# An encoder block on one core: value products of 256 columns in the attention, a smaller tile ring, the gated unit by token halves, and gate stores on another queue

## The chip, the cores and the metric

One core of a Trainium2 chip runs the whole program once. The metric is the device time of that execution in microseconds (us); lower is better. PE is the matrix engine, ACT the scalar engine, DVE the vector engine, POOL the GpSimd engine, SP the engine that here only issues DMAs. ACT and POOL issue DMAs too, each from its own instruction stream.

## The reference

```python
h = h + 0.5 * swiglu(rms_norm(h, g1), wg1, wu1, wd1)              # 1024 tokens x 1024
z = rms_norm(h, gm) @ w_in
q, k, v, s_in, gates = split(z)                                  # 512 each, gates 2 x 1024
y_attn = neighbourhood_attention(q, k, v, rpb) @ w_attn_out      # 8 heads, 16 x 64 grid, window 8 x 16
y = s5_scan(s_in, forward) + s5_scan(s_in, backward) + D * s_in  # diagonal state space
y = gelu(y); y_ssm = (y * sigmoid(y @ glu_w + glu_b)) @ w_ssm_out
h = h + (sigmoid(gates[0]) * y_attn + sigmoid(gates[1]) * y_ssm) @ w_out
h = h + 0.5 * swiglu(rms_norm(h, g2), wg2, wu2, wd2)
h = h + (p @ w_proj) * sigmoid(rms_norm(h, g3) @ w_gate)
return rms_norm(h, gf)
```

## The kernel before, in words

All products of weights are made from operands split into a high and a low part: `split` copies the value rounded (ACT, L159) and subtracts it (DVE, L160), and `mm3` issues three products of 512 columns (L190, L191, L192). A weight tile so split is called wh and wl.

The program is written as one main stream of such products and one side generator. After each `mm3` the main stream calls `tick()`; when the number that the generator last yielded has run down, the generator writes its next piece into the program. So `yield 3` means that three `mm3` of the main stream stand between two pieces. PE executes in the order written. The orders of ACT, DVE, POOL and SP are set by the scheduler of the compiling layer, which sorts by a simulated timeline; the build fixes them, and each engine then works through its list.

The first feed-forward layer ends near 685 us and the second one begins near 1327 us. Between them lies the mixer. Its main stream is the projection of q, k and the gates, 84 steps `s_run` of 12 products each (banks px, py, pz), in twelve groups of seven. A step needs a weight tile blk (loaded by a DMA on ACT's queue) as wh and wl. Results leave by `s_evac` into tiles z, and `s_out` stores the gates from z to g_d: four stores for each group of gates, on ACT's queue.

The generator `mixer_side` writes, in this order: the injection of the state-space input; the scan; the attention; the products that turn states into outputs (yo); the gated unit (glu).

The scan is 128 steps of three POOL instructions each (L1154, L1155, L1156), which depend on each other and on nothing else after the injection. `scan_steps` only writes them down; `scan["c"]` counts the steps that are written, not those that POOL has done.

The attention is 64 units, numbered 0 to 63 here, (head, row block, column block), in a loop over j. Iteration j writes the scores of unit j (bank s, tile sm), the three transpositions of unit j - 2 (`attn_turn`, bank pt), the value products of unit j - 4 (`attn_values`, bank O), then `yield 3`. The transposed weights are kept as a high part ph and a low part pl, two tiles of 384 columns. For each of three row groups, two value products of 128 columns are issued: v (high and low side by side, 128 columns of weights) times ph, and v's high part (64 columns) times pl. Four units share a bank O. When the fourth is in, ACT copies its lower half to ol (L1261), DVE adds (L1262) and the sum ot goes to o_d.

Tiles come from rings. Ring m has 24 buffers of 128 x 512 and holds blk, wh, wl, z, queries, values, ot, ol, y and more. Ring a has 12 buffers of 128 x 384 and holds sm, ph, pl, the bias tables tb, and before and after the attention the loads of the state-space products (ut, fmi, emi). A tile that takes a buffer waits until the last user of the buffer is done; if that was a store, until the store has landed.

After the attention, for each of 16 pairs, `ssm_load` brings emi (two DMAs) and ut; `ssm_out` copies states to xs, issues the yo products (L1180, L1182), copies them to ys (ACT, L1184) and stores them to y_d by two DMAs of POOL's queue (L1187). The gated unit works in two halves of the positions s: `glu_load` brings four tiles yt, each with half the positions of one channel quarter m, `glu_act` applies gelu in place on ACT, `glu_half` splits weight and yt to wgl, yh and yl and issues 12 products per quarter, then sigmoid and product give sg, stored to y2_d (named y_d in the rows). Every half needs all quarters, so the first half waits for the last pair of the state-space part.

At the end of the mixer `load_br` brings o_d and y2_d back by token halves t for the products br. The y2_d loads pick 64 of 128 chunks: runs of 256 bytes.

Of the kernel before, what the change touches and what calls it, by code (L numbers as in the profile page):

```python
# [16 lines left out]
P = 128  # L17
SEQ = 1024
# [23 lines left out]
def encoder_block(ctx, tc, I, out):  # L42
# [79 lines left out]
    o_d = dtile("o_d", [512, SEQ])  # L122
    g_d = dtile("g_d", [16, P, SEQ])
    y_d = dtile("y_d", [4, P, L, NCH])
    y2_d = dtile("y2_d", [512, SEQ])
    f_d = dtile("f_d", [NPAIR, P, 512])
    e_d = dtile("e_d", [NPD, P, 384])

# [937 lines left out]
    cur.update(st=(ap_, "k4", 2), w=(ap_, "m", NM), tmp=(ap_, "m", NM))  # L1066

    def ta(name, shape=(P, 384), dt=F32):
        return ap_.tile(list(shape), dt, tag="a", bufs=12, name=name)

    def proj(w, t, name):
        o = bank(name)
# [130 lines left out]
    def load_q(hd, rb):  # L1203
        hp, i = hd // 2, hd % 2
        qs[hd, rb] = [tmp("q" + n, dt=F32R) for n in "hl"]
        for a in range(2):
            for s_ in halves2:
                nc.sync.dma_start(qs[hd, rb][a][s_].bitcast(F32), q_d[hp, a, halves2[i], hsl(rb)])

    def load_v(hd, cb):  # L1210
        n = 4 * KNC[cb]
# [28 lines left out]
    def attn_turn(cb, sm):  # L1240
        kp = 4 * KNC[cb]
        tp = bank("pt")
        for g in range(3):
            T.transpose(tp[0:kp, ksl(g)], sm[:, g * kp:(g + 1) * kp], ident)
        ph, pl = ta("pth", dt=F32R), ta("ptl", dt=F32R)
        A.copy(ph[0:kp], tp[0:kp, 0:384])
        V.tensor_tensor(pl[0:kp], tp[0:kp, 0:384], ph[0:kp].bitcast(F32), ALU.subtract)
        return ph, pl

    def attn_values(hd, rb, cb, O, ph, pl):  # L1250
        kp = 4 * KNC[cb]
        hl = vld[hd, cb]
        for g in range(3):

            T.matmul(O[:, ksl(cb)], lhsT=hl[0:kp, rb + g], rhs=ph[0:kp, ksl(g)], start=(g == 0), stop=False,
                     skip_group_check=True)
            T.matmul(O[0:64, ksl(cb)], lhsT=hl[0:kp, rb + g, 0:64], rhs=pl[0:kp, ksl(g)], start=False, stop=(g == 2),
                     skip_group_check=True)
        if cb == 3:
            ot, ol = tmp("ot"), tmp("ol")  # L1260
            A.copy(ol[0:64], O[64:128])  # L1261
            V.tensor_tensor(ot[0:64].rearrange("p (r b c) -> p b r c", r=8, b=4),  # L1262
                            O[0:64].rearrange("p (b r c) -> p b r c", b=4, r=8),
                            ol[0:64].rearrange("p (b r c) -> p b r c", b=4, r=8), ALU.add)
            late.append((o_d[hd * 64:(hd + 1) * 64, hsl(rb)], ot[0:64]))


    ygs = {}

    def glu_load(t):  # L1270
        for m in range(4):
            yt = ygs[t, m] = tmp("yt")
            nc.sync.dma_start(yt, y_d[m, :, 4 * t:4 * t + 4].rearrange("p t c -> p (t c)"))

    def glu_act(t):
        for m in range(4):
            A.activation(ygs[t, m], ygs[t, m], AF.Gelu_apprx_tanh)
# [6 lines left out]
    def glu_w(raw):  # L1284
        w = ap_.tile([P, 2, HT], F32R, tag="k4", bufs=2, name="wgl")
        split(w[:, 0], w[:, 1], raw)
        return w

    def glu_half(t, raws):
        os_ = [bank("glu") for _ in range(4)]  # L1290
        for k in range(4):
            w = glu_w(raws.pop(0))
            y = tmp("yh", dt=F32R), tmp("yl", dt=F32R)
            split(*y, ygs[t, k])
            if 4 * t + k < 6:
                raws.append(glu_raw((k + 2) % 4))
            yield 2
            for m in range(4):
                mm3(os_[m], (w[:, 0, ksl(m)], w[:, 1, ksl(m)]), y, k == 0, k == 3)
        for m in range(4):  # L1300
            sg = tmp("sg")
            A.activation(sg, os_[m], AF.Sigmoid, bias=glub[:, m:m + 1])
            V.tensor_tensor(sg, sg, ygs.pop((t, m)), ALU.mult)
            nc.scalar.dma_start(y2_d[ksl(m), hsl(t)], sg)
        yield 2

    stored, ready = set(), set()
    SO = 56
# [1 line left out]
    def mixer_side():  # L1310
        yield from u_second()
        while 3 not in stored:
            yield 1
        yield 7
        new_x()
        ld = {}
        for pr in range(3):
            ld[pr] = inject_load(pr)
        yield 10
        for pr in range(NPAIR):  # L1320
            if pr + 3 < NPAIR:
# [17 lines left out]
        load_q(0, 0)  # L1339
        for _ in range(6):  # L1340
            scan_steps(1)
            yield 2
        sms, pts, O = {}, {}, {}
        late.clear()
        lo, so = {}, {}
        for j in range(n + 5):
            if j < n:
                hd, rb, cb = units[j]
                b = 2 * hd + rb
                load_tab(b + cb // 2, (1, 2, 0, 0)[cb]) if cb < 3 else None  # L1350
                if cb == 1 and rb == 0:
                    load_q(hd, 1)
                if cb == 1 and rb == 1 and hd + 1 < NH:
                    while hd + 1 not in ready:
                        yield 1
                    load_q(hd + 1, 0)
                if rb == 0 and cb == 2 and hd + 1 in ready:
                    load_k(hd + 1)
                if rb == 1 and cb == 2 and hd + 1 < NH and hd + 1 not in khl:
                    load_k(hd + 1)  # L1360
                sms[j] = attn_scores(hd, rb, cb)
            if 0 <= j - 2 < n:
                pts[j - 2] = attn_turn(units[j - 2][2], sms.pop(j - 2))
            while late:
                nc.scalar.dma_start(*late.pop())
            if 0 <= j - 4 < n:
                hd, rb, cb = units[j - 4]
                if cb == 0:
                    O[hd, rb] = bank("O")
                attn_values(hd, rb, cb, O[hd, rb], *pts.pop(j - 4))  # L1370
# [7 lines left out]
        scan_steps(NCH)  # L1378
        for p in range(NPAIR + 1):
            if 3 <= p + 3 < NPAIR:  # L1380
                lo[p + 3] = ssm_load(p + 3)
            if p < NPAIR:
                so[p] = ssm_out(p, *lo.pop(p))
            if p > 0:
                so.pop(p - 1)()
            yield 1 + p % 2
        yield 3
        glu_load(0)
        raws = [glu_raw(0), glu_raw(1)]
        yield 11  # L1390
        glu_act(0)
        glu_load(1)
        yield 2
        glu_act(1)
        for t in range(2):
            yield from glu_half(t, raws)

    start(mixer_side())

# [58 lines left out]
    def load_br(t, b):  # L1458

        res = []  # L1460
        if b == 0:
            for k in range(0, 4, 2):
                st = tst("br")
                nc.sync.dma_start(st.rearrange("p (k c) -> p k c", k=2),
                                  o_d[k * P:(k + 2) * P, hsl(t)].rearrange("(k p) c -> p k c", p=P))
                for i in range(2):
                    hi, lo = tx("bh"), tx("bl")
                    split(hi, lo, st[:, hsl(i)])
                    res.append((hi, lo))
            return res  # L1470
        for k in range(4):
            st = tmp("br")
            hi, lo = tx("bh"), tx("bl")
            mark["br"] = nc.sync.dma_start(st.rearrange("p (s c) -> p s c", s=L),
                                           y2_d[ksl(k)].rearrange("p (s c) -> p s c", s=L)[:, :, t * 64:(t + 1) * 64]).ins
# [131 lines left out]
    s_store()  # L1607


    ap_cm.__exit__(None, None, None)  # L1610
    lp = ctx.enter_context(tc.tile_pool(name="lt", bufs=1, reuse_waits="tile"))
    cur.update(tmp=(lp, "m", 17), w=(lp, "w", 20))
# [345 lines left out]
```

## Time and profile before

| what | value |
|---|---|
| median of 3 runs | 2091.4 us (2090.44 to 2091.76) |
| the profiled execution | 2089.91 us, of which the span of its instructions is 2088.1 us |
| mean granted PE clock | 0.996 |
| PE busy | 2053.6 us, 98% of the span |
| PEld / DVE / ACT / POOL busy | 80% / 70% / 48% / 22% |
| first and last score product of the attention | 825.9 and 1035.9 us |
| first and last value product | 837.7 and 1047.6 us |
| yo products | 1052.6 to 1090.1 us |
| glu products | 1104.9 to 1140.9 us |
| first br product | 1157.8 us |

Times within the execution are us from the start of the span. A matrix product's listed duration (389 ns for 512 columns) contains its way through the array, so the pace of a stream is read from the distance between two starts. Idle time in brackets behind a row is that of its engine just before it, with what ended it.

### The profile page before, as it was taken

Reading aid. Unit: us, or ns where it says so; the run is one execution under the profiler, and the core shown is the slowest. Engines: PE = TensorE matmul, PEld = TensorE weight load, DVE = VectorE, ACT = ScalarE, POOL = GpSimd, SP = SyncE. Lnnn points to the kernel's source line nnn. Section 1 sums busy time; section 2 is a strip of 40 time slices with the busy share of each in tenths; the row PEclk is TensorE's granted clock in tenths of the full one; section 3 lists DMA queues with packets and bytes.
Section 4 is the critical chain, followed back from the end, with each engine's and each line's share of the span. In section 5 each row is a group of like instructions: output and inputs, shape, how many; then the busy total and the mean of one; then the engine's idle time right before and its main releaser. Section 6 shows DMA issues by size and latency. Waiting matters only on the chain.

```text
span 2088.1 us, 28214 instructions
## 1 busy us (share of the span) xinstructions
PE 2053.6 (98%) x9518; PEld 1680.4 (80%) x9518; DVE 1468.1 (70%) x2478; ACT 1010.5 (48%) x1878; POOL 468.4 (22%) x688
## 2 busy tenths in 40 slices
PE   9999999999999998999999999999999999999998
PEld 3788888888888887887887788788888888888887
DVE  7897777667867846677645668986665665786855
ACT  6434333344445434677755545543333334445544
POOL 0037556441000508888230001000000000000000
PEclk9999999999999999999999999999999999999999
DMA  3434444475533567677585875243324238533302
GB/s 133 144 119 152 128 134 121 145 258 179 191 105 121 144 179 221 198 232 222 183 273 172 266 242 119 78 148 122 97 86 139 81 120 296 157 107 91 120 22 81
DMA packets 214512, 319.75 MB, mean 153 GB/s; under 512 B 37856, under 2 KB 81504, under 8 KB 214368
## 3 DMA queue, kind: packets, MB, share of 16 engines
q1 hardware_dynamic: 173840, 258.14, 39.2%
q10 hardware_dynamic: 36368, 52.46, 7.5%
q0 software_dynamic: 4160, 7.36, 1.6%
q8 instruction: 75, 1.23, 0.2%
q14 instruction: 69, 0.57, 0.1%
HBM read 224.01 MB, written 93.85 MB: 152 GB/s over the span
## 4 chain that ended last, share of the span: by engine, by line
PE 86%; DVE 6%; DMA 5%; ACT 2%; issue 1%; ACTq 0%; SPq 0%; DVEq 0%
PE dx L190 4%; PE dx L191 4%; PE dx L192 4%; PE gx L190 3%; PE ux L190 3%; PE ux L192 3%; PE gx L191 3%; PE gx L192 3%; PE ux L191 3%; PE dy L191 2%; PE dy L192 2%; PE dy L190 2%; DMA blk<-in_win 2%; PE uy L190 2%; PE gy L190 2%; PE uy L192 2%
## 5 line engine op out<-in xcount | busy, mean ns | idle before, releaser
L159 ACT CAST wh<-hbuf 128x512 fp32r<-128x512 f32 x280 | 173.0, 622 | 389.2 <-PE gx L191 84.6
L160 DVE TENSOR_TENSOR wl<-hbuf,wh 128x512 fp32r<-128x512 f32 x280 | 217.4, 779 | 122.9 <-ACT wh L159 120.8
L159 ACT CAST wh<-wblk 128x512 fp32r<-128x512 f32 x190 | 118.1, 622 | 187.2 <-PE dx L191 81.9
L160 DVE TENSOR_TENSOR wl<-wblk,wh 128x512 fp32r<-128x512 f32 x190 | 130.8, 691 | 50.7 <-ACT wh L159 43.2
L190 PE MATMUL dx<-ah,wh 128*128 128x512 f32 x416 | 163.5, 393 | 0.4 <-DVE hbuf L694 0.3
L192 PE MATMUL dx<-ah,wl 128*128 128x512 f32 x416 | 161.9, 389 | 0.0
L191 PE MATMUL dx<-al,wh 128*128 128x512 f32 x416 | 161.9, 389 | 0.0
L160 DVE TENSOR_TENSOR al<-araw,ah 128x512 fp32r<-128x512 f32 x154 | 106.6, 696 | 50.7 <-PE dx L191 18.3
L190 PE MATMUL gx<-xh,wh 128*128 128x512 f32 x320 | 125.0, 391 | 1.2 <-DVE c L581 1.2
L190 PE MATMUL ux<-xh,wh 128*128 128x512 f32 x320 | 125.0, 391 | 0.0
L192 PE MATMUL ux<-xh,wl 128*128 128x512 f32 x320 | 124.5, 389 | 0.0
L192 PE MATMUL gx<-xh,wl 128*128 128x512 f32 x320 | 124.5, 389 | 0.0
L191 PE MATMUL gx<-xl,wh 128*128 128x512 f32 x320 | 124.5, 389 | 0.0
L191 PE MATMUL ux<-xl,wh 128*128 128x512 f32 x320 | 124.5, 389 | 0.0
L159 ACT CAST ah<-araw 128x512 fp32r<-128x512 f32 x154 | 95.0, 620 | 46.4 <-PE dx L191 14.2
L1154 POOL TENSOR_TENSOR sc<-X,rho 128x128 f32<-128x128 f32 x128 | 82.4, 644 | 59.4 <-ACT X L1137 49.4
L190 PEld LDWEIGHTS dx<-ah,wh 128*128 128x128 f32 x416 | 78.1, 188 | 18.7 <-DVE hbuf L694 1.2
L428 DVE TENSOR_TENSOR hbuf<-hbuf 128x512 f32<-128x512 f32 x120 | 90.5, 755 | 2.1
L191 PEld LDWEIGHTS dx<-al,wh 128*128 128x128 f32 x416 | 78.1, 188 | 16.7 <-issue 0.7
L160 DVE TENSOR_TENSOR wl<-blk,wh 128x512 fp32r<-128x512 f32 x84 | 60.9, 727 | 43.4 <-ACT wh L159 42.9
L192 PEld LDWEIGHTS dx<-ah,wl 128*128 128x128 f32 x416 | 78.1, 188 | 16.2
L190 PE MATMUL px<-xh,wh 128*128 128x512 f32 x192 | 78.7, 410 | 3.4 <-ACT z L1539 2.6
(398 smaller groups left out, 5741.6 us busy)
## 6 DMA issues: line engine op xcount, KB each, us to landing
araw<-a_d SPq DMA_DIRECT2D x154, 256.0 KB
a_d<-c SPq DMA_DIRECT2D x148, 256.0 KB
wblk<-in_wd SPq DMA_DIRECT2D x88, 256.0 KB
hbuf<-in_wg SPq DMA_DIRECT2D x40, 512.0 KB
hbuf<-in_wu SPq DMA_DIRECT2D x40, 512.0 KB
blk<-in_win ACTq DMA_DIRECT2D x48, 256.0 KB
hbuf<-in_xT SPq DMA_DIRECT2D x32, 256.0 KB
h_d<-hbuf ACTq DMA_DIRECT2D x32, 256.0 KB
```

The lines of the kernel that those rows point to most:

```text
L159: A.copy(hi, src)
L160: return eng.tensor_tensor(lo, src, hi.bitcast(F32), ALU.subtract)
L190: T.matmul(o, lhsT=wh, rhs=xh, start=first, stop=False, skip_group_check=more)
L191: T.matmul(o, lhsT=wh, rhs=xl, start=False, stop=False, skip_group_check=more)
L192: T.matmul(o, lhsT=wl, rhs=xh, start=False, stop=last, skip_group_check=more)
L428: V.tensor_tensor(b11, (b12, b22, None, None, b21)[i - 2], b11, ALU.subtract)
L1154: G.tensor_tensor(sc, both, rho4, ALU.mult)
```

## The change

1. The high and the low part of the transposed weights lie in one tile of two times 384 columns. One product of 256 columns per row group takes both (three per unit in place of six, each with 128 columns of weights). Two units share a bank O. After each pair of units ACT copies a quarter (64 x 256) to ol, and DVE makes three adds (one of 64 x 256, two of 64 x 128).
2. Ring a is a pool of its own that is closed and opened again: 12 buffers before the attention, then 6 of 384 columns and 3 of 768 (the weights), then 12 again from iteration j = n + 4 on, the last one, where now the first three `ssm_load` stand (before: iterations n, n + 1, n + 2).
3. The two parts of the queries are loaded in two iterations; the keys one iteration later. Every eighth iteration yields 4 in place of 3.
4. The gated unit works by token halves. Each quarter m is loaded (two tiles) as soon as its four pairs are stored, three of four inside the loop over pairs, and gelu runs there too. Weight and y of a step are split one step ahead. y2_d has the layout [2, 4, 128, 512], one contiguous tile per load.
5. In `s_out` the gate stores go to POOL's queue once all scan steps are written: 24 of 32 stores.

```diff
-    y2_d = dtile("y2_d", [512, SEQ])
+    y2_d = dtile("y2_d", [2, 4, P, HT])
...
+        return pools["as"].tile(list(shape), dt, tag="a", bufs=pools["na"], name=name)
+    def part(n):
+        if "ac" in pools:
+            pools.pop("ac").__exit__(None, None, None)
+        if n:
+            pools["ac"] = tc.tile_pool(name="as", bufs=1, reuse_waits="tile")
+            pools["as"], pools["na"] = pools["ac"].__enter__(), n
+    part(12)
...
-        ph, pl = ta("pth", dt=F32R), ta("ptl", dt=F32R)
-        A.copy(ph[0:kp], tp[0:kp, 0:384])
-        V.tensor_tensor(pl[0:kp], tp[0:kp, 0:384], ph[0:kp].bitcast(F32), ALU.subtract)
+        pt = pools["as"].tile([P, 2, 384], F32R, tag="pt", bufs=3, name="pth")
+        A.copy(pt[0:kp, 0], tp[0:kp, 0:384])
+        V.tensor_tensor(pt[0:kp, 1], tp[0:kp, 0:384], pt[0:kp, 0].bitcast(F32), ALU.subtract)
...
-            T.matmul(O[:, ksl(cb)], lhsT=hl[0:kp, rb + g], rhs=ph[0:kp, ksl(g)], start=(g == 0), stop=False, ...)
-            T.matmul(O[0:64, ksl(cb)], lhsT=hl[0:kp, rb + g, 0:64], rhs=pl[0:kp, ksl(g)], start=False, stop=(g == 2), ...)
+            T.matmul(O[:, c * 256:(c + 1) * 256], lhsT=hl[0:kp, rb + g], rhs=pt[0:kp, :, ksl(g)],
+                     start=(g == 0), stop=(g == 2), skip_group_check=True)
+        if c == 1:
+            o = O.rearrange("p (b x c) -> p b x c", b=2, x=2)
+            ol = ta("ol")[0:64, 0:256].rearrange("p (b c) -> p b c", b=2)
+            A.copy(ol, o[64:128, :, 0])
+            V.tensor_tensor(ol, o[0:64, :, 1], ol, ALU.add)
+            dst = ot[0:64].rearrange("p (r b c) -> p b r c", r=8, b=4)
+            for i in range(2):
+                V.tensor_tensor(dst[:, cb - 1 + i], o[0:64, i, 0]..., ol[:, i]..., ALU.add)
...
+    def glu(raws):
+        steps = [(t, k) for t in range(2) for k in range(4)]
+        nxt = glu_prep(0, 0, raws)
+        yield 2
+        for n, (t, k) in enumerate(steps):
+            w, y = nxt
+            if k < 3:
+                nxt = glu_prep(*steps[n + 1], raws)
             for m in range(4):
                 mm3(os_[m], (w[:, 0, ksl(m)], w[:, 1, ksl(m)]), y, k == 0, k == 3)
...
+                    nc.scalar.dma_start(y2_d[t, m], sg)
+            yield 2 + k % 2
...
+        part(6)
...
             scan_steps(2)
-            if j >= n:
-                if j - n < 3:
-                    lo[j - n] = ssm_load(j - n)
-            yield 3
+            if j == n + 4:
+                part(12)
+                for p in range(3):
+                    lo[p] = ssm_load(p)
+            yield 3 + (j % 8 == 7)
         scan_steps(NCH)
...
+            if p in (6, 10, 14):
+                glu_load((p - 6) // 4)
+            if p in (10, 14):
+                glu_act((p - 10) // 4)
...
+        glu_load(3)
         yield 3
+        glu_act(2)
+        yield 4
+        glu_act(3)
+        yield from glu(raws)
...
-            mark["br"] = nc.sync.dma_start(st.rearrange("p (s c) -> p s c", s=L),
-                                           y2_d[ksl(k)].rearrange("p (s c) -> p s c", s=L)[:, :, t * 64:(t + 1) * 64]).ins
+            nc.sync.dma_start(st, y2_d[t, k])
...
-            later.append((nc.scalar, g_d[2 * m + second, :, hsl(t)], src))
+            later.append((nc.gpsimd if scan["c"] >= NCH else nc.scalar, g_d[2 * m + second, :, hsl(t)], src))
```

On POOL the list of the kernel before ends the scan and goes on with the stores of ys. In all three excerpts the number behind a name tells tiles apart, and the square bracket names what an instruction waits for: an engine's count, or the landing of a DMA (DMAHW: issued by SP or ACT; DMASW: issued by POOL).

```order
L1154 TENSOR_TENSOR sc_6135<-X_6590,rho_1128 128x128 [waits Pool_49]
L1155 TENSOR_TENSOR sc_6135<-sc_6135 128x64 [waits Pool_49]
L1156 TENSOR_TENSOR X_6590<-sc_6135,X_6590 128x32x2 [waits Pool_49]
L1187 DMA y_d_86<-ys_10766 8x16x128 [waits Activation_49]
L1187 DMA y_d_86<-ys_10766 8x16x128
```

In the changed kernel the same place reads so; the three lines of a scan step are now L1164, L1165 and L1166, and the last of the 128 steps ends in the last scan row here.

```order
L1584 DMA g_d_85<-z12_9624 128x512 [waits DVE_49]
L1164 TENSOR_TENSOR sc_6138<-X_6593,rho_1128 128x128 [waits Pool_49]
L1165 TENSOR_TENSOR sc_6138<-sc_6138 128x64 [waits Pool_49]
L1166 TENSOR_TENSOR X_6593<-sc_6138,X_6593 128x32x2 [waits Pool_49]
L1164 TENSOR_TENSOR sc_6138<-X_6593,rho_1128 128x128 [waits Pool_49]
L1165 TENSOR_TENSOR sc_6138<-sc_6138 128x64 [waits Pool_49]
L1166 TENSOR_TENSOR X_6593<-sc_6138,X_6593 128x32x2 [waits Pool_49]
L1164 TENSOR_TENSOR sc_6138<-X_6593,rho_1128 128x128 [waits Pool_49]
L1584 DMA g_d_85<-z22_9581 128x512 [waits DVE_49]
L1165 TENSOR_TENSOR sc_6138<-sc_6138 128x64 [waits Pool_49]
L1166 TENSOR_TENSOR X_6593<-sc_6138,X_6593 128x32x2 [waits Pool_49]
L1584 DMA g_d_85<-z11_9529 128x512 [waits DVE_49]
```

The first gate store that moved to POOL stands behind step 125 of the scan, the second inside step 128, the rest behind it.

On ACT, around the evacuation of the same group of gates (the third of the eight), the kernel before reads:

```order
L1235 ACTIVATE sm_9777,stat_9778<-sm_9777,stat_9778 128x384 [waits DVE_49]
L1506 DMA blk_9804<-in_win 128x512 [waits DMAHW6_49]
L1237 ACTIVATE sm_9777<-sm_9777,stat_9778 128x384 [waits DVE_49]
L159 CAST wh_9807<-blk_9336 128x512
L1549 DMA g_d_85<-z12_9752 128x512 [waits DMAHW0_49,DVE_49]
L1246 CAST pth_9832<-pt_9828 96x384 [waits PE_49]
```

And the changed kernel (L1245 is exp, L1247 the scaling by the sum, L1256 the copy of the transposed weights):

```order
L1541 DMA blk_9751<-in_win 128x512 [waits DMAHW1_49]
L159 CAST wh_9753<-blk_9626 128x512 [waits DMAHW6_49]
L1256 CAST pth_9779<-pt_9775 96x384 [waits PE_49]
L1245 ACTIVATE sm_9769,stat_9770<-sm_9769,stat_9770 128x384 [waits DVE_49]
L159 CAST wh_9795<-blk_9626 128x512 [waits DMASW4_49,DVE_49]
L1247 ACTIVATE sm_9769<-sm_9769,stat_9770 128x384 [waits DVE_49]
L1256 CAST pth_9815<-pt_9811 128x384 [waits PE_49]
L1270 COPY ol_9821<-O_9782 64x256 [waits DMAHW7_49,PE_49]
```

The store is gone from ACT, and wh_9795 takes over the buffer of z12_9624: its DMASW4 is the landing of POOL's store of z12_9624 shown above. sm_9769, the tile behind it, belongs to unit 46.

On ACT at the gated unit, the kernel before and then the changed kernel, where yt_11137 and yt_11138 hold quarter m = 3 and yt_10844 and yt_10845 hold m = 0:

```order
L1277 ACTIVATE yt_11283<-yt_11283 128x512 [waits DMAHW5_49]
L159 CAST yh_11308<-yt_11209 128x512 [waits Activation_49]
L1277 ACTIVATE yt_11285<-yt_11285 128x512 [waits DMAHW6_49]
L1506 DMA blk_11318<-in_win 128x512 [waits DMASW5_49,DMASW4_49,Activation_49]
L1277 ACTIVATE yt_11287<-yt_11287 128x512 [waits DMAHW7_49]
```

```order
L159 CAST wh_11169<-blk_11108 128x512 [waits DMAHW4_49,DMASW1_49,DMASW0_49]
L1289 ACTIVATE yt_11137<-yt_11137 128x512 [waits DMAHW6_49,DMASW5_49,DMASW4_49]
L1289 ACTIVATE yt_11138<-yt_11138 128x512 [waits DMAHW7_49]
L159 CAST yh_11184<-yt_10844 128x256
L159 CAST yh_11184<-yt_10845 128x256
```

Before, one gelu of the second half stands ahead of the first split yh; now both gelus of the last quarter do.

More of the change, by code (lines that the diff above doesn't have):

```diff
@@ L1201, in load_k, with load_q @@
             nc.sync.dma_start(t[s_].bitcast(F32), k_d[hp, a, halves2[i]])
-    def load_q(hd, rb):
+    def load_q(hd, rb, a):
         hp, i = hd // 2, hd % 2
[L1205 to L1208, printed above, removed]
+        q = tmp("q" + "hl"[a], dt=F32R)
+        qs.setdefault((hd, rb), []).append(q)
+        for s_ in halves2:
+            nc.sync.dma_start(q[s_].bitcast(F32), q_d[hp, a, halves2[i], hsl(rb)])
     def load_v(hd, cb):
@@ L1251, in attn_values @@
+        return pt
+    def attn_values(hd, rb, cb, O, ot, pt):
         kp = 4 * KNC[cb]
         hl = vld[hd, cb]
+        c = cb % 2
         for g in range(3):
[L1255 to L1258, printed above, removed]
-        if cb == 3:
[L1260 to L1264, printed above, removed]
+            T.matmul(O[:, c * 256:(c + 1) * 256], lhsT=hl[0:kp, rb + g], rhs=pt[0:kp, :, ksl(g)],
[7 more added lines that the diff above has]
+            for i in range(2):
+                V.tensor_tensor(dst[:, cb - 1 + i], o[0:64, i, 0].rearrange("p (r c) -> p r c", r=8),
+                                ol[:, i].rearrange("p (r c) -> p r c", r=8), ALU.add)
+        if cb == 3:
@@ L1265, in attn_values, with glu_load @@
             late.append((o_d[hd * 64:(hd + 1) * 64, hsl(rb)], ot[0:64]))
     ygs = {}
[L1270 to L1277, printed above, removed]
+    def glu_load(m):
+        ygs[m] = [tmp("yt") for _ in range(2)]
+        for i in range(2):
+            nc.sync.dma_start(ygs[m][i], y_d[m, :, 4 * i:4 * i + 4].rearrange("p s c -> p (s c)"))
@@ L1279, in glu_raw, with glu_act, glu_parts @@
+    def glu_act(m):
+        for y in ygs[m]:
+            A.activation(y, y, AF.Gelu_apprx_tanh)
+    def glu_parts(t, m, *xs):
+        for i in range(2):
+            yield (ygs[m][i].rearrange("p (s c) -> p s c", s=4)[:, :, t * 64:(t + 1) * 64],
+                   *(x[:, i * 256:(i + 1) * 256].rearrange("p (s c) -> p s c", s=4) for x in xs))
     def glu_raw(k):
@@ L1282, in glu_raw, with glu_prep @@
         return raw
-    def glu_w(raw):
+    def glu_prep(t, k, raws):
         w = ap_.tile([P, 2, HT], F32R, tag="k4", bufs=2, name="wgl")
[L1286 to L1297, printed above, removed]
+        split(w[:, 0], w[:, 1], raws.pop(0))
+        y = tmp("yh", dt=F32R), tmp("yl", dt=F32R)
+        for src, hi, lo in glu_parts(t, k, *y):
+            split(hi, lo, src)
+        if 4 * t + k < 6:
+            raws.append(glu_raw((k + 2) % 4))
+        return w, y
+    def glu(raws):
[4 more added lines that the diff above has]
+            w, y = nxt
+            if k == 0:
+                os_ = [bank("glu") for _ in range(4)]
+            if k < 3:
+                nxt = glu_prep(*steps[n + 1], raws)
             for m in range(4):
                 mm3(os_[m], (w[:, 0, ksl(m)], w[:, 1, ksl(m)]), y, k == 0, k == 3)
[L1300 to L1305, printed above, removed]
+            if k == 3:
+                for m in range(4):
+                    sg = tmp("sg")
+                    A.activation(sg, os_[m], AF.Sigmoid, bias=glub[:, m:m + 1])
+                    for src, o in glu_parts(t, m, sg):
+                        V.tensor_tensor(o, o, src, ALU.mult)
+                    nc.scalar.dma_start(y2_d[t, m], sg)
+                    if m == 0 and t == 0:
+                        nxt = glu_prep(1, 0, raws)
+            yield 2 + k % 2
     stored, ready = set(), set()
@@ L1338, in mixer_side @@
         load_k(0)
-        load_q(0, 0)
+        load_q(0, 0, 0)
+        load_q(0, 0, 1)
         for _ in range(6):
@@ L1350, in mixer_side @@
                 load_tab(b + cb // 2, (1, 2, 0, 0)[cb]) if cb < 3 else None
-                if cb == 1 and rb == 0:
-                    load_q(hd, 1)
-                if cb == 1 and rb == 1 and hd + 1 < NH:
+                if cb < 2 and rb == 0:
+                    load_q(hd, 1, cb)
+                if cb < 2 and rb == 1 and hd + 1 < NH:
                     while hd + 1 not in ready:
                         yield 1
-                    load_q(hd + 1, 0)
-                if rb == 0 and cb == 2 and hd + 1 in ready:
+                    load_q(hd + 1, 0, cb)
+                if rb == 0 and cb == 3 and hd + 1 in ready:
                     load_k(hd + 1)
@@ L1367, in mixer_side @@
                 hd, rb, cb = units[j - 4]
+                if cb % 2 == 0:
+                    O[0] = bank("O")
                 if cb == 0:
-                    O[hd, rb] = bank("O")
-                attn_values(hd, rb, cb, O[hd, rb], *pts.pop(j - 4))
+                    O[1] = tmp("ot")
+                attn_values(hd, rb, cb, O[0], O[1], pts.pop(j - 4))
                 if rb == 1 and hd + 1 < NH:
@@ L1385, in mixer_side @@
                 so.pop(p - 1)()
+            if p in (6, 10, 14):
+                glu_load((p - 6) // 4)
+            if p in (10, 14):
+                glu_act((p - 10) // 4)
+            if p >= NPAIR - 1:
+                raws.append(glu_raw(p - NPAIR + 1))
             yield 1 + p % 2
+        glu_load(3)
         yield 3
[L1388 to L1396, printed above, removed]
+        glu_act(2)
+        yield 4
+        glu_act(3)
+        yield from glu(raws)
     start(mixer_side())
```

5 lines of the change are left out of this document (2 added, 3 removed).

## The prediction

> **What bounds the kernel now.** I read the busy times, then the stretch of the attention, then what PE waited for between the first score and the last br product.
>
> ```profile
> PE 2053.6 (98%) x9518; PEld 1680.4 (80%) x9518; DVE 1468.1 (70%) x2478; ACT 1010.5 (48%) x1878; POOL 468.4 (22%) x688
> 826.00:1053.00 227.00, 219.78 (x1331) 189.04 (x1329) 159.64 (x393) 159.05 (x367) 154.04 (x305) 1.00 0.70 214
> PE pt L1244 <- ACT sm L1237: 5.6, 5, 2.6
> PE br L190 <- ACT bh L159: 2.1, 1, 2.1
> PE glu L190 <- ACT yh L159: 1.6, 1, 1.6
> PE glu L191 <- DVE yl L160: 1.1, 2, 0.9
> PE br L191 <- DVE bl L160: 0.2, 1, 0.2
> ```
>
> PE is the bound. In the attention it works 219.8 of 227 us, DVE and ACT 159 each. So work taken off PE shortens the run if nothing else falls behind. One engine there has a clock of its own:
>
> ```profile
> L1154 POOL TENSOR_TENSOR sc<-X,rho x128: 490/530/1777, 779.4 to 1002.2; 128x128 f32<-128x128 f32 x128
> 998.90 0.36 POOL L1156 TENSOR_TENSOR X<-sc,X 128x64 f32<-128x64 f32 x1
> 1000.35 0.36 POOL L1156 TENSOR_TENSOR X<-sc,X 128x64 f32<-128x64 f32 x1
> ...
> 1003.55 0.32 POOL L1156 TENSOR_TENSOR X<-sc,X 128x64 f32<-128x64 f32 x1
> ```
>
> The scan begins at 779.4 and takes 1.75 us a step (222.8 us for 127 starts), whatever PE does, as it waits for no PE result. Step 128 ends at 1003.9, step 125 (the 998.90 row, three rows of this line before the last) at 999.3. Before, nothing in the attention waits for POOL.
>
> **Value products.** The chain of waits in the middle of the attention, and two rows of the only stream of 256 columns, at the end of the kernel:
>
> ```profile
> 933.70 7.75 DMA blk<-in_win
> ...
> 941.54 0.85 DVE blk L428
> 942.39 0.47 DVE ptl L1247
> ...
> 942.96 0.62 ACT sm L1237
> ...
> 943.62 0.55 PE pt L1244 x3
> 944.17 0.06 PE O L1255
> ...
> 944.64 0.28 PE py L190
> 944.92 0.24 PE py L191
> 2062.40 0.28 PE L192 MATMUL pg<-xh,whl 128*128 128x256 f32 x1
> 2062.52 0.28 PE L190 MATMUL pg<-xh,whh 128*128 128x256 f32 x1
> ```
>
> Six products last from 944.17 to 944.64, and the next product takes 0.28 for its usual 0.23: 0.52 us. Three of 256 columns at 0.12 make 0.36. Saved: 0.16 x 64 units = 10.3 us, all on PE. Bounds: 0.14 each while the weights change would leave 6; no weight loading at all, half of the 0.23 of 512 columns, gives 11.5.
>
> The Trainium skill ("TensorE: Matmul & The Clock Gate", Back-to-back issue gap) gives N/2.4 + 2.5 ns between products without their weight loads: 56 ns at 128 columns, 109 at 256, so 0.33 us for either form, and by it the change would save about half a microsecond here. The rows above differ, so the sum goes by them.
>
> **The additions.** The copies and adds of the banks double in number:
>
> ```profile
> L1262 DVE TENSOR_TENSOR ot<-O,ol 64x512 f32<-64x512 f32 x16 | 10.9, 680 | 5.5 <-ACT ol L1261 5.5
> ```
>
> Estimated from this 0.68 for 512 columns, with half of it fixed: 0.5 for 256, 0.4 for 128, so 2.6 us in place of 0.7 per four units, 31 us of DVE over the attention. DVE idles 67 of 227 us there, which covers it; without that cover up to 31. The ring of 6 holds what the 12 held beside the weights; at its tightest three tables, three sm. I cost it at 0, bounds -2 and +5.
>
> **The gate stores on POOL.** ACT sheds 24 DMA issues. But a POOL store has its place behind the scan steps written ahead of it: the first, of z12_9624, behind step 125, and ACT's cast wh_9795 waits for its landing. The chain above shows what such a head of a list does: one late blk held DVE at 941.5, ptl and the reciprocal behind it came late, then sm, and PE stood 2.6 us. Here ACT is held, and sm of unit 46 stands behind. On POOL no row shows a DMA behind a scan step.
>
> The Trainium skill ("TensorE: Matmul & The Clock Gate", Part 1, on engine queue depths) calls ACT, DVE and GpSimd strict FIFO; for DVE the chain above agrees.
>
> When does PE need it?
>
> ```profile
> 987.57 0.49 PE L1244 MATMUL pt<-ident,sm 128*128 128x128 f32 x3
> L159 ACT CAST wh<-blk 128x512 fp32r<-128x512 f32 x53 | 32.8, 618 | 9.3 <-DMA ql<-q_d 3.0 <-DMA tb<-in_tabs 2.0 <-ACT qkh L1522 1.8
> L1237 ACT ACTIVATE sm<-sm,stat 128x384 f32<-128x384 f32 x32 | 19.6, 616 | 20.1 <-DVE stat L1236 20.1
> s_d<-s POOLq DMA_DIRECT2D x4, 256.0 KB, 3.1
> ```
>
> The first row is unit 46's transposition. Ahead of it 44 units' value products have shrunk (-7.1), and six longer yields put 18 more products of 0.23 there (+4.1): PE arrives at 984.6. The store leaves at 999.3, lands 3.1 later (the only 256 KB stores of POOL in the trace), then cast and scaling, 0.62 each: 1003.6. **PE stands 19 us.** It does not help to be faster or slower before; POOL sets this time. The price hangs on the scan's pace: a step in a calm moment takes 1.45 (998.90 to 1000.35), and from 985 on DVE stands still, worth 0.3 for each of nine steps; a busier DVE before that may cost as much. Bounds 1000 and 1007, so 15 to 23 us. Behind it SP holds a load (vhl) for the second store, which lands near 1007; its user comes 12 us after unit 46, so nothing.
>
> Long waits also cost clock:
>
> ```profile
> 1106.50:1109.90 3.40, 3.40 (x10) 2.63 (x9) 1.36 (x2) 1.24 (x3) 0.00 (x0) 0.50 0.31 83
> 1168.00:1171.40 3.40, 3.40 (x8) 2.70 (x9) 3.17 (x4) 3.40 (x4) 0.00 (x0) 0.50 0.00 0
> ```
>
> After the glu and the br wait PE ran 3.4 us at half clock, losing 1.7. After 19 us I count one and a half such stretches, 2.5 us; bounds 1.7 and 5.
>
> **State-space loads.** The first emi now waits for the last add of the attention. A load on SP's queue:
>
> ```profile
> 983.85 3.37 DMA ql<-q_d
> ```
>
> Copy 0.4, adds 1.3, three issues of 0.3, 3.4 to land: 6.0 us behind the last value product; PE has 21 products, 4.8 us. 1.2 us late; bounds 0 and 4.
>
> **Gated unit.** What the last pair had to pass before:
>
> ```profile
> 1090.43 0.38 ACT L1184 COPY ys<-yo 128x256 f32<-128x256 f32 x1 [0.40 <-ACT wh L159]
> 1091.21 1.18 POOL L1187 DMA_DIRECT2D y_d<-ys  x2 [0.23 <-issue]
> 1098.21 0.64 ACT L1277 ACTIVATE yt<-yt 128x512 f32<-128x512 f32 x1
> ```
>
> The first half's last quarter had come 7.8 us after the last yo. The same way now ends in two gelus (1.3) and two half splits (0.4 each), which all stand ahead of the first glu product: 9.9. PE gets there after 30 products, 6.8: a wait of 3.1. The gelu of m = 2 may also stand ahead of the last ys, up to 1.3. I take 3.5. The waits of 1.6 and 1.1 go, since splits run a step ahead: net +0.8, bounds -2.7 and +3; the half clock stays.
>
> **Branches.**
>
> ```profile
> 1147.96 8.17 SPq L1474 DMA_DIRECT2D br<-y_d  x6
> 1160.03 1.92 SPq L1464 DMA_DIRECT2D br<-o_d  x1
> 1166.52 6.17 ACT L159 CAST bh<-br 128x512 fp32r<-128x512 f32 x7 [3.13 <-DMA br<-o_d]
> ```
>
> Six loads of short runs kept SP busy for 8 us, and o_d, behind them, came late. Six contiguous issues at 0.3 take 2, so o_d comes 6 us sooner, and the waits of 2.1 and 0.2 go with their half clock: -4.0, bounds -4 and 0.
>
> **Sum.** -10.3 + 19.0 + 2.5 + 1.2 + 0.8 - 4.0 = +9.2 us. The profiled execution took 2089.9 (2088.1 and 1.8 around it), so 2099.1; the median of the runs stands 1.5 above it: 2100.6, I say 2100.
>
> **Rivals.**
> - Faster: the store gates nothing, because the scan is past step 125 before PE needs unit 46. For it: POOL's calm pace of 1.45. At that pace throughout, step 125 would end at 961. Against: 222.8 us for 127 steps, under much the same DVE load. The time: -10.3 + 1.2 + 0.8 - 4.0 = -12.3, 2079. The whole stays at par if the stall is 9.8 us, that is if the store lands by 993 in place of 1002.4: a pace of 1.68.
> - Even: the stall is there, but scan and landing are quick (1000) and the glu wait goes entirely: +9.2 - 4 - 3.5 = +1.7, 2093.
> - Slower still: after the stall, tables, values and stores come late together, the half clock lasts 5 us, and the br wait stays, as its o_d loads also wait for wst's buffers: +9.2 + 2.5 + 4 = +15.7, 2107.
> - The new products are no cheaper (the formula's case): +9.2 + 10 = 2110.
>
> **Chances.** Forecast (2096 to 2105) 0.53; faster 0.16; even 0.12; slower still 0.15; no cheaper products 0.04. A measurement of this kernel tells 0.2%, 4.2 us, from no change. So faster 0.16, same 0.12, slower 0.72. The range leaves out most of the faster case below and the last below 2110 above: 2083 to 2108; the forecast's own is 2096 to 2105.
>
> **What would show it.** Right: one gap of 15 to 23 us on PE at a transposition near 985, ACT there idle until a POOL DMA lands near 1002; value products three per unit, 0.12 apart; a wait at the first glu product, none at br L190. Wrong: the scan ending near 990, or ACT's cast wh not waiting; then the time is near 2079, and the step that failed is the pace of POOL.

## The result and the profile after

The changed kernel takes 2104.9 us (median of 4 runs, 2103.2 to 2106.0) against 2091.6 of the kernel before (4 runs, 2090.4 to 2092.9): ratio 1.0063, 95% interval 1.0045 to 1.008. It is 13.4 us slower. The forecast was 2100 in a range of 2083 to 2108. The profiled execution has a span of 2104.2 us, 16.1 more than that of before.

The page, the stretch of the attention, and what PE waited for, first up to the attention's end and then behind it:

```profile
PE 2047.3 (97%) x9326; PEld 1671.8 (79%) x9326; DVE 1481.8 (70%) x2574; ACT 1012.9 (48%) x1902; POOL 481.3 (23%) x712
826.00:1053.00 227.00, 201.26 (x1068) 171.11 (x1069) 160.29 (x441) 151.16 (x358) 161.81 (x317) 0.95 0.66 198
PE pt L1254 <- ACT sm L1247: 23.4, 8, 16.2
...
PE yo L1190 <- DMA ut<-u_d: 2.4, 1, 2.4
PE glu L190 <- ACT yh L159: 2.3, 1, 2.3
PE py L190 <- ACT z L1574: 1.3, 1, 1.3
PE yo L1192 <- DVE xs L1184: 0.8, 1, 0.8
```

PE has 6 us less work than before and the run is longer: it stands. One wait of 16.2 us holds most of it, where before the longest was 2.6. No wait at br is left. Around that wait, first POOL's rows, then ACT's, then PE's:

```profile
1002.43 0.36 POOL L1166 TENSOR_TENSOR X<-sc,X 128x64 f32<-128x64 f32 x1
1002.73 0.57 POOL L1584 DMA_DIRECT2D g_d<-z  x1
...
988.10 0.19 ACT L1245 ACTIVATION_READ_ACCUMULATOR sm<-sm,stat 128x1 f32 x1
1005.12 0.62 ACT L159 CAST wh<-blk 128x512 fp32r<-128x512 f32 x1 [16.83 <-DMA g_d<-z]
1005.64 0.61 ACT L1247 ACTIVATE sm<-sm,stat 128x384 f32<-128x384 f32 x1
...
1006.31 0.90 PE L1254 MATMUL pt<-ident,sm 128*128 128x128 f32 x3 [16.16 <-ACT sm L1247]
```

This is the chain that the prediction named, link by link: step 125 of the scan, the store behind it, its landing 2.3 us later, the cast, the scaling, the transposition. The store left at 1002.7 (forecast 999.3), and PE, which came to the transposition at 990.1 (984.6), went on at 1006.3 (1003.6). The 3 us at the store are not in the pace: the scan began at 782.7 in place of 779.4 and took the same 220 us to step 125.

Where the 16.1 us of the two profiles lie, by the first and last starts on PE (main-stream products that the longer yields moved from one stretch to another are taken off at 0.227 each):

| stretch | before | after | difference, like for like |
|---|---|---|---|
| up to the first score | 825.9 | 828.8 | +2.9 |
| first score to last value product | 221.8 | 238.8 | +11.5 (24 products more) |
| to the first yo product | 4.9 | 7.5 | +2.6 |
| yo products | 37.5 | 40.5 | +3.0 |
| to the first glu product | 14.9 | 11.0 | +2.3 (27 fewer) |
| glu, and on to br | 52.9 | 52.1 | -1.4 (3 more) |
| br products | 91.7 | 86.8 | -4.9 |

The first row can't be put down to one part. In the profiles of the six kernels with the new ring that stretch ended between 827.8 and 830.7, in those of the eight with the old one between 825.9 and 827.9, so some of it may be the ring's; no run tried it. In the attention three things make the 11.5: -10.0 of shorter value products; +17.4 of waits (24.6 us in place of 7.2, of which the one wait is 16.2); and +4.1 of half clock, where before there was none (PE worked 8.3 us of this stretch at half clock: 4.9 behind the long wait, as the last section shows, and 3.4 from 932.7 on, behind a wait of 3.0).

### The profile page after: what moved, and what is told of

It reads as the page before. It is cut to its first block, busy times and chain, and to the rows that moved or that the text cites. A ratio compares the mean times of both kernels' runs of the same rounds, so it can differ in the third digit from the quotient of the medians.

```text
span 2104.2 us, 27984 instructions
## 1 busy us (share of the span) xinstructions
PE 2047.3 (97%) x9326; PEld 1671.8 (79%) x9326; DVE 1481.8 (70%) x2574; ACT 1012.9 (48%) x1902; POOL 481.3 (23%) x712
## 4 chain that ended last, share of the span: by engine, by line
PE 78%; POOL 9%; DVE 5%; DMA 3%; issue 2%; ACT 2%; SPq 0%; ACTq 0%; DVEq 0%
PE dx L190 4%; PE dx L191 4%; PE dx L192 4%; POOL sc L1164 4%; PE ux L190 3%; PE gx L190 3%; PE ux L191 3%; PE ux L192 3%; PE gx L192 3%; PE gx L191 3%; POOL X L1166 3%; POOL sc L1165 3%; PE dy L191 2%; PE dy L190 2%; PE dy L192 2%
## 5 line engine op out<-in xcount | busy, mean ns | idle before, releaser
L159 ACT CAST ah<-araw 128x512 fp32r<-128x512 f32 x154 | 94.8, 619 | 48.4 <-PE dx L191 14.2
L1164 POOL TENSOR_TENSOR sc<-X,rho 128x128 f32<-128x128 f32 x128 | 80.8, 632 | 60.0 <-ACT X L1147 50.1
L428 DVE TENSOR_TENSOR hbuf<-hbuf 128x512 f32<-128x512 f32 x120 | 89.7, 748 | 2.1
```

The source lines that it names most:

```text
L159: A.copy(hi, src)
L428: V.tensor_tensor(b11, (b12, b22, None, None, b21)[i - 2], b11, ALU.subtract)
L1164: G.tensor_tensor(sc, both, rho4, ALU.mult)
```

## The experiments

Each was timed beside the kernel before. That kernel itself ran between 2087.5 and 2100.7 us, so the ratios with their intervals count, and the microseconds against before are worked out from the ratio and 2091.

**The POOL queue.** Four kernels: the stores back on ACT; the stores on POOL as the only change; and a scan cut short, which lets the first store go sooner.

```diff
# act_store, on the changed kernel
-            later.append((nc.gpsimd if scan["c"] >= NCH else nc.scalar, g_d[2 * m + second, :, hsl(t)], src))
+            later.append((nc.scalar, g_d[2 * m + second, :, hsl(t)], src))
# only_pool: the reverse, on the kernel before
# scan_118 (and scan_112, with 16), on the changed kernel
+            if c < NCH - 10:
                 G.tensor_tensor(sc, both, rho4, ALU.mult)
...
```

> The changed kernel with one line undone: all 32 gate stores on ACT's queue. Theory (the store stands behind step 125 of the scan on POOL, and ACT's cast behind it holds PE): the wait of 16.2 us at a transposition near 1006 is gone, with it some 2 us of half clock: 2104.9 - 18 = 2087, 4 to 5 us below the kernel before. Rival 1 (the smaller ring or the doubled additions make PE wait there, the store is only what shows last): the wait stays over 8 us, 2097 or more. Rival 2 (the wait is refilled: ACT, with its 24 issues back, falls behind elsewhere): 2091 to 2095, several waits of 1 to 3 us at transpositions.

> The kernel before with only the gate stores moved to POOL's queue. There the first two stores stand behind step 128 (1003.9 in the profile of before), and the copy of z21 on ACT (994.8 there) waits for the landing of the second; the scaling sm stands two places behind it. Theory: PE waits from about 997 until 1003.9 + 0.6 + 0.6 + 2.5 + 1.8 = 1009, 12 us, and 2 us of half clock: 2091.5 + 14 = 2105 (2101 to 2109). Rival 1 (the new ring and the value products cause the wait): no such wait, 2091.5 as before.

> The changed kernel without the last 10 of the 128 scan steps (the states of the last ten positions are left out); the gate stores stay on POOL, the first one now behind step 118, the lists of ACT, DVE, PE and SP are the same. In the changed kernel step 118 ended at 992.9, step 125 at 1002.8. Theory: the store leaves 9.9 us sooner, the wait shrinks from 16.2 to 6.3 us, and with less half clock the time is 2094 to 2096. Rival 1 (ring or additions): the wait stays at 16, 2105. Rival 3 (a store on POOL's queue is slow by itself, wherever it stands): 2103 to 2105.

> As the run with 118 steps, but with the last 16 steps left out: the first store stands behind step 112, which ended at 982.3, and lands near 985, before ACT comes to the cast (988.3) and PE to the transposition (990.2). Theory: no wait there, about 2087, the same within 1 us as with the stores on ACT's queue, though 24 stores still go by POOL. Rival 3 (POOL's queue itself): over 2095.

| run | ratio to before | interval | us against before | longest wait at a transposition |
|---|---|---|---|---|
| changed kernel | 1.0063 | 1.0045 to 1.008 | +13.2 | 16.2 |
| only_pool | 1.0055 | 1.0041 to 1.0069 | +11.5 | 13.0 |
| act_store | 1.0009 | 0.9999 to 1.0019 | +1.9 | 3.2 |
| scan_118 | 1.0024 | 1.0014 to 1.0033 | +5.0 | 3.2 |
| scan_112 | 1.0028 | 1.0018 to 1.0038 | +5.9 | 3.1 |

Here is only_pool, POOL first, then ACT and PE:

```profile
1003.96 0.33 POOL L1156 TENSOR_TENSOR X<-sc,X 128x64 f32<-128x64 f32 x1
1004.22 1.65 POOL L1549 DMA_DIRECT2D g_d<-z  x3
...
1007.54 0.59 ACT L1516 COPY z<-px 128x512 f32<-128x512 f32 x1 [14.16 <-DMA g_d<-z]
...
1009.21 0.90 PE L1244 MATMUL pt<-ident,sm 128*128 128x128 f32 x3 [13.05 <-ACT sm L1237]
```

The wait needs neither the new ring nor the new products: the move alone makes one of 13.0 us, ending at 1009.2 as worked out (1009), and costs 11 us. With the stores back on ACT it is gone. The two cut scans say that the long wait comes from the place behind the scan and not from POOL's queue: 24 stores still go there, and the long wait is gone. Neither came out as worked out (times by the ratios). scan_118 met its time, 2096.0, but not its mechanism: its scan came to step 118 at 987.6 and not at 992.9, and left no wait of 6 us. So the two runs are one case and no scale. scan_112 was expected at 2087 and came to 2096.9, over the 2095 that was set for a queue that is slow by itself. Since act_store, with no store on POOL, stands at 2092.9, 3 to 4 us remain between it and the cut scans, with intervals that overlap a little. Whether POOL's queue costs them is left open, as these runs also take work off POOL.

act_store missed too, and this is the larger surprise: 2087 was expected and 2094 came (+2, interval 0 to +4). Without its worst wait the change gains nothing. The waits come back in small, and the clock with them (in the second row, the stretch of the attention, it is the third number from the end):

```profile
PE pt L1254 <- ACT sm L1247: 13.0, 11, 3.2
826.00:1053.00 227.00, 212.23 (x1116) 178.83 (x1117) 167.80 (x463) 158.49 (x375) 156.74 (x308) 0.98 0.68 202
```

There are eleven waits at transpositions of 13.0 us in all, where before there were five of 5.6, and the mean clock is 0.98 in place of 1.00. From the first score to the last value product all waits of PE grew by 6.9 us over the kernel before, and PE worked 9.8 us at half clock, which costs 4.9: together they outweigh the 10.0 that the value products save. Time and waits are those of rival 2; its reason, ACT's 24 issues, is not it, since scan_112, with these issues on POOL, has ten such waits of 11.9.

**The parts one by one.** To see which part costs or fails to pay, each alone on the kernel before. val_only has the products of 256 columns with the additions and the ring; ring_only the ring with the old products and sums:

```diff
# ring_only, on val_only: ph and pl are the halves of the tile pt
-            T.matmul(O[:, c * 256:(c + 1) * 256], lhsT=hl[0:kp, rb + g], rhs=pt[0:kp, :, ksl(g)], ...)
+            T.matmul(O[:, ksl(cb)], lhsT=hl[0:kp, rb + g], rhs=ph[0:kp, ksl(g)], ...)
+            T.matmul(O[0:64, ksl(cb)], lhsT=hl[0:kp, rb + g, 0:64], rhs=pl[0:kp, ksl(g)], ...)
...
-            ol = ta("ol")[0:64, 0:256].rearrange("p (b c) -> p b c", b=2)
+            ot, ol = tmp("ot"), tmp("ol")
# no_low, on the kernel before
-            T.matmul(O[0:64, ksl(cb)], lhsT=hl[0:kp, rb + g, 0:64], rhs=pl[0:kp, ksl(g)], ...)
```

> The kernel before with the value products of 256 columns, their adds and their ring alone (emi loads late with them; queries, yields, gated unit and gate stores as before). With the stores on ACT the whole change came to 2094 where the sum said 2079: some 13 us are missing, most of them in the attention. Theory P (work taken off PE there is worth its time, and the other parts cost more than I thought): 2091 - 10.3 + 2 (late emi) = 2083. Theory W (PE only runs into ACT, DVE and the blk loads sooner, so the waits at the transpositions grow): 2088 to 2092. Theory R (ring of 6 and 3, or the additions): 2088 to 2095, and the two next runs tell it from W.

> The kernel before without the value products of the low part of the weights (three of the six products of a unit are left out; the copies, the subtraction and the ring are as before). It takes about 0.18 us a unit off PE, 11 us, and touches nothing else. Theories P and R: 2080, and no more waits than before. Theory W: 2085 or more, with 4 us or more of new waits and half clock between the first score and the last value product.

> The kernel before with the ring laid out anew alone (6 buffers, 3 for the pairs of weights, the state-space loads at the last iteration), six value products of 128 columns and the sums as before. Theory R, ring: waits at transpositions or scores grow by 5 us, 2096 to 2100. Theory W or P: only the late emi, 2 us, 2093.

> The kernel before with the gated unit by token halves and the contiguous y2_d alone. From the ledger of the changed kernel with the stores on ACT: br -4.9, the wait at the first glu product +2.5 over before (it was 4.2 there, 1.6 before), no waits within glu -1.1, yo products +1. Together -2.5: 2088 to 2089. If the glu wait of 4.2 came only from the gate stores or the late start there, -4: 2087.

| run | ratio to before | interval | us against before |
|---|---|---|---|
| val_only | 1.0040 | 1.0028 to 1.0052 | +8.4 |
| no_low | 1.0001 | 0.999 to 1.0012 | +0.2 |
| ring_only | 1.0014 | 1.0004 to 1.0024 | +2.9 |
| glu_only | 1.0019 | 1.0007 to 1.0032 | +4.0 |

no_low decides: three of the six value products of a unit are left out (0.367 in place of 0.548 us, 11.6 us over 64 units), nothing else is touched, and the time stays. Theory W holds: PE only comes sooner to the same point. In the profile its waits from the first score to the last value product are 17.8 us, where before they were 7.2, and 6.8 us of its work ran at half clock, where before none did. What PE and DVE wait for there:

```profile
PE pt L1244 <- ACT sm L1237: 15.3, 12, 3.4
...
DVE blk L428 <- DMA blk<-in_win: 18.9, 7, 4.8
DVE wl L160 <- ACT wh L159: 11.0, 15, 2.3
DVE sm L1232 <- DMA tb<-in_tabs: 9.2, 9, 2.2
DVE blk L430 <- DMA blk<-in_win: 7.8, 4, 3.1
```

PE stands at transpositions for sm; sm waits for DVE; and DVE, whose list is worked off in order, stands at blk and at the tables tb: 35.9 us for loads in these three rows, where before the same three held 15.2, 2.9 and 3.2.

val_only is worse than expected under any theory, 5 us above ring_only. What differs is seen on SP's queue. The waits of the table loads (L1230) and of the tables' user, val_only first, then ring_only's longest row of L1230:

```profile
SPq L1230 <- PE pt L1254: 42.2, 22, 6.6
...
DVE sm L1242 <- DMA tb<-in_tabs: 13.1, 5, 4.8
```

```profile
SPq L1230 <- DVE stat L1242: 29.3, 18, 3.7
```

In ring_only a table takes a buffer that DVE's addition has freed. In val_only the tile ol takes two buffers of the same ring of six in every four units, so a table gets one that the transposition, two iterations later, must free first: the trace names it as what released the load. Tables come late, DVE waits for them, and PE behind it. This is read from the waits; no run puts ol back into the other ring.

**What paces the attention.** If loads do, sooner or fewer loads must show it. On no_low:

```diff
# no_low_early
-    LL, LP = 4, 2
+    LL, LP = 5, 2
# no_low_no_tables
-            tabs[b, v] = ta("tb")[:, 0:n]
-            nc.sync.dma_start(tabs[b, v], I["tabs"][b, :, TOFF[v]:TOFF[v] + n])
+            tabs[b, v] = U["a11"][0][0][:, 0:n].bitcast(F32)
```

> As the run without the low products (11 us of PE work left out, 0 us gained), but the weight blocks blk are loaded one step of the main stream sooner (LL = 5 in place of 4, some 4 us). In the run without the low products DVE stood 26.7 us for blk and 9.2 us for the tables, and PE 18 us behind that. Theory W1 (PE now outruns the landing of blk): DVE's wait for blk falls under 12 us, PE's waits in the attention to 10 us or less, and the time to 2084 to 2088. Theory W2 (the wait is in the length of the chains on ACT and DVE, whatever lands): 2091 to 2095, blk waits turn into others. Rival (the ring of 24 has no room for a fifth load): the loads' issue does not get earlier, 2093 or more.

> As the run without the low products, and besides the 45 loads of the bias tables are left out (the addition reads a tile that already lies in the core in place of a table; same instructions on PE, DVE and ACT). This takes 7 MB of some 46 MB and 45 places on SP's queue out of the attention, and frees ring a. Open so far: 11 us less on PE there gave nothing, and sooner blk loads only moved DVE's waits to tables and queries. Theory L (loads pace the attention: transfer, SP's order or the rings behind them): from first score to last value product 218 us or less in place of 226, DVE's waits for loads halved, 2083 to 2087. Theory C (the chains of copies, adds and exp on ACT and DVE pace it): 223 us or more there, 2091 to 2095, the waits then on ACT and DVE results.

no_low_early: 1.0008 (0.9997 to 1.0018), no gain. DVE's waits for blk fell (L428 from 18.9 to 16.4, L430 from 7.8 to 1.3) and PE's at transpositions too, from 15.3 to 8.3, near what theory W1 asked. But DVE's wait for tables went from 9.2 to 14.0, two waits for queries appeared on PE, and PE worked 12.6 us of the attention at half clock in place of 6.8:

```profile
DVE blk L428 <- DMA blk<-in_win: 16.4, 7, 3.5
DVE sm L1232 <- DMA tb<-in_tabs: 14.0, 8, 2.4
...
DVE blk L430 <- DMA blk<-in_win: 1.3, 1, 1.3
PE pt L1244 <- ACT sm L1237: 8.3, 7, 1.9
PE s L1228 <- DMA ql<-q_d: 5.0, 2, 3.4
```

no_low_no_tables: 0.9936 (0.9921 to 0.9952), 2078.5 us, 13 below the kernel before, with which no_low stood level. The attention, from the first score (s) to the last value product (O), and the waits at transpositions; no_low first, then without the tables:

```profile
L1255 PE MATMUL O<-pth,vhl x192: 223/277/456, 839.6 to 1053.5; 96*128 96x128 f32 x96, 128*128 128x128 f32 x96
L1228 PE MATMUL s<-khl,qh x64: 292/338/359, 827.5 to 1040.8; 128*128 128x288 f32 x32, 128*128 128x384 f32 x32
```

```profile
L1254 PE MATMUL O<-pth,vhl x192: 220/277/328, 839.9 to 1036.6; 96*128 96x128 f32 x96, 128*128 128x128 f32 x96
L1227 PE MATMUL s<-khl,qh x64: 292/318/341, 827.9 to 1025.6; 128*128 128x288 f32 x32, 128*128 128x384 f32 x32
PE pt L1243 <- ACT sm L1236: 2.8, 3, 1.6
```

226.0 us become 208.7 (the kernel before had 221.8), with the same instructions on PE, DVE and ACT. PE's waits at transpositions fall from 15.3 to 2.8, DVE's for loads in the three rows from 35.9 to 17.0. The time is even lower than theory L's 2083 to 2087. So theory L is shown for no_low: once PE has less to do, loads pace the attention. That in the kernel before PE's 97% hid a second limit about equally long is concluded from it; the kernel before with fewer loads alone was not run. The run takes away three things at once, 7 MB of transfer, 45 places on SP's queue and buffers of ring a; which of them binds is not told apart.

**Two small parts.**

> The kernel before with the third part of the change alone: queries in two iterations, keys one later, every eighth iteration yields 4. By the other runs this part must be worth much: new products and ring alone +8, gated unit alone +4, all parts with the stores on ACT +2; if the parts add up, this one gives 8 + 4 - 2 = 10 us, 2082. If its worth lies only in giving the smaller ring room (tables and sm loaded in another order), it gives nothing here: 2090 to 2093.

> The kernel before with y2_d laid out [2, 4, 128, 512] alone; the gated unit works as before, so each of its 8 stores becomes two of 256-byte runs and the 8 loads of the branches are contiguous. My term for the branches, alone: -4 (the waits of 2.1 and 0.2 and the half clock go): 2087. In every run with the contiguous layout so far the br products took 86.8 us, in place of 91.7. If the short runs only change their place (the stores land late, so the first loads do), 2091 or more.

queries_yields: 0.9995 (0.9986 to 1.0004). Alone it is worth nothing. So the parts don't add: alone they come to +8.4, +4.0 and -1.0, all together with the stores on ACT to +1.9. That this part recovers beside the small ring what that ring loses is a guess that no run tried. y2_layout: 1.0017 (1.0006 to 1.0028), 3.5 us slower and not 4 faster. Its br products still take 92.0 us (1164.2 to 1256.2), with the wait at another place:

```profile
PE glu L190 <- ACT yh L159: 4.5, 2, 2.5
PE br L190 <- DVE gt L1654: 2.4, 1, 2.4
```

The wait for o_d is gone as I reasoned, but the gate tile gt comes late next, and the doubled stores delay glu. In queries_yields, on the other hand, br takes 86.8 us with the old layout. So the contiguous tiles are neither enough nor needed for the 4.9; what they do in the whole change is not settled.

None of the kernels with the full computation is measurably faster than before.

## Why the prediction was right, and where it was not

The sign, the place and the cause held, and the time lay within the range, 5 us above the forecast. Between the two profiles the sum's +9.2 stands against +16.1. The attention came to 11.5 (forecast -10.3 + 19 + 2.5 = 11.2); the missing 7 us lie in front of it (+2.9) and around the yo products (2.6 and 3.0, forecast 1.2 in all), less 0.9 at the branches. That the attention came out so near is in part luck: in run time the stall was worth half of its price, and the gain it was set against does not come without the stall.

- **The gate stores on POOL.** Right in mechanism, shown from both sides. PE waited 16.2 us (forecast 19, bounds 15 to 23) and lost 2.4 more at half clock (forecast 2.5): it came to the wait 5.5 us later than forecast and left it 2.7 later. The step that was mis-sized is what this costs in run time: 19 + 2.5 in the sum, 11 in both pairs of runs (2104.9 against 2094.0, and only_pool). In the changed kernel the long wait stands in part where short ones would: besides it the attention has 8.4 us of waits and 3.4 us of half clock, while act_store has 14.1 and 9.8. That loads run ahead while PE stands, and so spare it these, is argued, not shown. only_pool doesn't support it: its other waits there are as before (7.1 and 7.2), its profile is 14.2 us longer, and its 11.5 has an interval of 8.6 to 14.4.
- **Value products.** Right in size on PE, and worth nothing in time. A group of three and two products behind it, after:

```profile
953.02 0.60 PE L1265 MATMUL O<-pth,vhl 128*128 128x256 f32 x3
953.46 0.40 PE L190 MATMUL pz<-xh,wh 128*128 128x512 f32 x1
953.70 0.39 PE L191 MATMUL pz<-xl,wh 128*128 128x512 f32 x1
```

A group of six, before:

```profile
947.12 0.30 PE L1255 MATMUL O<-pth,vhl 96*128 96x128 f32 x1
...
947.67 0.44 PE L190 MATMUL py<-xh,wh 128*128 128x512 f32 x1
947.95 0.40 PE L191 MATMUL py<-xl,wh 128*128 128x512 f32 x1
```

From the group's start to the next product's start it is 0.44 in place of 0.55, and that next product itself takes 0.24 in place of 0.28. Together (medians over all 64 units) that is 0.675 in place of 0.832, so 0.157 a unit and 10.0 us of PE, where the prediction had 10.3. Its two readings were each 0.08 too low, and the slips cancel: beyond the usual 0.23 of the next product the old group costs 0.60 and not 0.52, the new one 0.45 and not 0.36. The new products do follow one another in 0.12, but the first, behind the transposition, takes 0.20. By the formula in the Trainium skill ("TensorE: Matmul & The Clock Gate", Back-to-back issue gap), which counts no weight loads, half a microsecond would have been left; the measured 10.0 does not agree with it.

The step that failed is an earlier one: "PE is the bound ... so work taken off PE shortens the run if nothing else falls behind". no_low shows that 11.6 us off PE gain nothing, since DVE and the transpositions then wait for loads, and act_store that the 10.0 come back as waits and half clock.
- **The additions and the ring, at 0.** Failed: val_only costs 8 us. Of the ring the prediction said "at its tightest three tables, three sm"; it left out ol, which now lives there too. By ring_only the ring alone accounts for 3; the other 5 came with the new products, their additions and ol in the ring. The additions took 28.4 us of DVE there, where before they took 10.9: 17.5 more, not the estimated 31. Whether that time has a part in the 5 was not tried.
- **State-space loads.** Right place, too small: PE waited 2.4 us, not 1.2, since the load of ut took 4.5 from issue to landing, not 3.4.
- **Gated unit.** +0.9 together for +0.8, near in part by luck: PE waited 2.3 at the first glu product (forecast 3.5), but also 1.3 at py shortly before it, for ACT's copy of z, which the prediction did not have. The yo products, which I left alone, grew by 3.0. Of this 1.7 is a stretch of half clock (1076.1 to 1079.5) behind the late ut and 0.8 a wait for xs. The gelu between the pairs can cost there too: in glu_only, 4 us slower alone, PE stood 2.7 us for xs while ACT waited for yt ahead of its first gelu.
- **Branches.** -4.9 for -4.0. The waits went as forecast, but whether by the contiguous loads is not settled, as y2_layout and queries_yields show.
- **The rivals.** "Faster", 2079, was no such case: with no long wait at all the change runs at 2094, 15 off. Its price rested on the same two steps, PE as the bound and the ring at 0. The even point, a stall of 9.8 us, was wrong with it: there is no stall short enough to make the change gain.

## What to carry to other kernels

A DMA on a compute engine's queue has a place in that engine's list: ask what is ahead of it when it is due, and who waits for its landing. An engine that is 97% busy in a stage is not proven to be its only bound: where DVE already waits for loads in the same stage (here 21 us in three rows), leave some of the bound's work out and look, before paying for a rewrite. When a ring is made smaller, count every tile that turns in it, and whose end frees the buffer that a load takes.

## What the runs showed of the hardware

The half clock came in stretches of 3.4 us, and how long PE stood did not alone decide on them. In the changed kernel, from the start of the long wait on (behind the window stand its length and the time that PE worked; the third number from the end is the granted clock):

```profile
990.20:994.10 3.90, 0.00 (x0) 0.00 (x0) 0.41 (x3) 0.00 (x0) 3.27 (x9) 1.00 0.26 64
994.20:1006.30 12.10, 0.00 (x0) 0.00 (x0) 0.53 (x1) 1.18 (x3) 10.21 (x27) 0.50 0.06 22
1006.30:1011.20 4.90, 4.89 (x15) 4.12 (x16) 4.01 (x12) 4.25 (x11) 3.27 (x6) 0.50 0.58 179
1011.20:1014.60 3.40, 3.40 (x20) 2.92 (x19) 2.10 (x7) 2.30 (x6) 0.00 (x0) 1.00 0.83 256
```

Half clock was granted 4 us after PE had stopped and lasted 17.1 us, five times 3.4. PE worked 4.9 us of it and lost 2.4; after the waits of 1.6 and 2.1 us at glu and br in the kernel before it lost 1.7 each. The wait of 2.6 us before 943.6, in the kernel before, cost none (this row is of that kernel):

```profile
943.60:947.00 3.40, 3.38 (x22) 2.98 (x23) 1.72 (x6) 3.10 (x8) 2.90 (x6) 1.00 0.58 176
```

The Trainium skill ("TensorE: Matmul & The Clock Gate", What's actually happening) describes a free-running window of about 3.4 us; the lengths of 3.4 and 17.1 agree, and that two like waits are charged differently fits a window that does not start with them.

POOL's scan steps took 1.42 us while DVE stood (991 to 1002 in the changed kernel) and 1.75 in the mean. The starts of two steps there:

```profile
991.51 0.51 POOL L1164 TENSOR_TENSOR sc<-X,rho 128x128 f32<-128x128 f32 x1
992.93 0.51 POOL L1164 TENSOR_TENSOR sc<-X,rho 128x128 f32<-128x128 f32 x1
```

The Trainium skill ("SBUF — State Buffer", SBUF: two separate sides) tells of a port pair that DVE and GpSimd hold in turn; these two numbers agree with it, but no run here takes the two apart.
